# Two transformer blocks on one core: the values products of block 2 turned round, GpSimd remainders cut in quarters, whole heads prepared ahead in block 1

## The chip, the core and the metric

The kernel runs on one NeuronCore of a Trainium2 chip. The metric is the device time of one execution in microseconds (us). TensorE (PE) multiplies matrices, VectorE (DVE) and ScalarE (ACT) do elementwise work and may read PSUM, GpSimd (POOL) does elementwise work on SBUF alone, and SyncE (SP) issues most of the transfers. Matrix products land in eight PSUM banks of 128 partitions by 512 float32 values.

## What is computed

The reference runs two transformer blocks, one after the other, on one sequence of 512 tokens with 1024 channels, in float32. Cut to what matters here:

```python
def first_block(x, ...):
    xn = rmsnorm(x, norm_mix_g)
    proj = xn @ w_in                                   # q, k, v, u, v-gate, forget logits
    att = forgetting_attention(q, k, v, log_f)         # 8 heads of 64, causal
    sg = chunked_spatial_gating(u, vg, ...)
    x = x + concatenate([att, sg]) @ w_out
    return rmsnorm(x + conv_ffn(rmsnorm(x), w_up, conv_w, conv_b, w_down))

def second_block(x, c, positions, ...):
    h = modulate(rmsnorm_2(x, g_attn_norm), sh_a, sc_a)
    q_lat, kv_lat, k_rope, ca_qkv = split(h @ w_in)
    o_mla = mla_attention(q, k, v)                     # 8 heads, keys of 96, values of 64
    o_ca = chunk_attention(cq, ck, cv, rel_bias)       # 8 heads of 64
    x = x + g_a * (concatenate([o_mla, o_ca]) @ w_out)
    ...                                                # a convolutional feed-forward part
```

In both blocks a head's attention is a softmax over the scores of 512 queries by 512 keys of which a causal part is allowed, and its product with v:

```python
s = einsum('bqhd,bkhd->bhqk', q, k) * scale + bias     # masked
p = softmax(s)
o = einsum('bhqk,bkhd->bqhd', p, v)
```

## The kernel before

**Products.** Channels stand on the partitions and the 512 tokens along the free dimension. A weight piece of 128 by up to 1024 values is loaded by a transfer (`load_split`, L337), cast by ACT to a rounded high part `whi` (L350), and the rest `wlo` is a subtraction (L351), on DVE, or on POOL for those pieces whose row in the plan says `pool=True`: twelve pieces, of w_u, w_qk and of w_ck1 and w_cv1. A step of a matrix product is then three PE instructions (hi by hi, hi by lo, lo by hi), all recorded at L372 (`mm`).

**Order.** The PE order is that of the code. The other engines' instructions are ordered by priority. The loop `attention()` (L619) runs over steps t; a step is one block of 128 queries of one head (four steps to a head, 32 to the first eight heads of a block). Step t issues the scores of t (`strip_scores`: PE products into a bank `s`, on DVE the bias at L597, on ACT the exponential at L601 into a tile `p`), some background work `bg` for DVE, ACT and POOL, then `fill.run(r / 2)`, then the turn of step t-1 (`strip_turn`: PE transposes of `p` at L610 back into its bank `s`, and one copy to a tile `pt` at L612, on an engine of the scheduler's choice, `nc.any`), `fill.run(r / 2)` again, what `later` holds, and the values of step t-2 (`strip_values`). `fill` is a list of jobs of PE work (the weight products of the neighbouring parts); `rate(t)` says how many nanoseconds of it go beside step t. Where fill has run dry, the steps follow each other without it.

**Values.** For a block of queries, `strip_values` multiplies for every block of keys the 128x128 block of `pt`, as stationary operand, with 64 columns of v: 1, 2, 3 and 4 products for the four steps of a head, into a 64-column piece of the bank `o`, which a pair of heads share. After a pair, `pair_end` (L709) divides by the sums (L715, L717, on DVE), and in the next step PE transposes the result into a bank `s` (L725), and `split` (L741 on ACT, L742 on DVE) makes of it one of the eight pairs `mix` that the output product `w_out` reads. Each head of 64 channels has its q and k as `qs`, `kh`, `kl` tiles with high and low halves stacked on the partitions (`stack_q`, `stack_k`; the second halves of kh and kl are copied by two transfers on SP, L700).

**Block 1** (L1266, `head`): a head's preparation comes in four slices, spread over the steps before its first. On POOL stand there the remainders `wlo`, the gelu of the gating part (L1111, L1112), its squares (L1124), the mask `cm` (L1277) and the gains (L1138). **Block 2** (`block2_mix`, L1361): eight heads of the chunked attention (`ca_head`, v in `vc`), then eight of the latent attention (`mla_head`, v in `vm`). The fill there is, in order, cq1, ck1, mla0, cv1, mla1, out0, out1 and the output's tail; its products leave PSUM by `nc.any` copies (L1462, L1463, L1469, L1521, L1526, L1597). Normalizing of q and k (`ca_norm` with the multiply L1457, `q_norm`, `k_norm`, `rope`) is background work. `gemm_tm`, `weave` and `then` make jobs of products and evacuations. PSUM banks: in block 1 three `s`, one `o`, four `mm`; in block 2 the same numbers.

Of the kernel before, what the change touches and what calls it, by code (L numbers as in the profile page):

```python
# [236 lines left out]
class Kernel:  # L237
# [99 lines left out]
    def load_split(self, src, pool, dest, skew):  # L337
# [281 lines left out]
    def attention(self, heads, fill, rate, bg, bgrate, mix, depth=1):  # L619
# [21 lines left out]
        for t in range(n + depth + 3):  # L641
            r = rate(t)
            if t < n:
# [3 lines left out]
                for h in range(len(heads)):  # L647
# [5 lines left out]
            u = t - depth  # L653
            if 0 <= u < n:
                h, qi = seq[u]
                pt[u] = self.strip_turn(hd[h], qi, sc.pop(u))
            if t > n + depth:
# [3 lines left out]
            fill.run(r / 2)  # L661
            for f in later:
                f()
            later = []
            u -= 1
            if 0 <= u < n:
                h, qi = seq[u]
                if u % 8 == 0:
                    o = self.bank("o")
                ov = 2 * qi + h % 2  # L670
                self.strip_values(hd[h], qi, pt.pop(u), o[:, ov * 64:(ov + 1) * 64])
                if h < last:
                    if u % 8 == 7:
                        later = [self.pair_end(o, mix, *hd[h]["end"])]
                elif u % 4 == 3:
                    later = [self.pair_end(o, mix, *hd[h]["end"], half=u % 8 // 4)]
# [12 lines left out]
    def stack_k(self, tiles, k, odd, scale=None):  # L689
        nc, (_, kh, kl) = self.nc, tiles  # L690
        a, b = HALF_P[::-1] if odd else HALF_P
        if scale is None:
            nc.scalar.copy(kh[a], k[a])
            nc.vector.tensor_tensor(out=kl[a], in0=k[a], in1=kh[a].bitcast(F32), op=ALU.subtract)
        else:
            nc.scalar.activation(out=kh[a], in_=k[a], func=AF.Copy, scale=scale[a])
            nc.vector.scalar_tensor_tensor(out=kl[a], in0=k[a], scalar=scale[a], in1=kh[a].bitcast(F32),
                                           op0=ALU.mult, op1=ALU.subtract)
# [10 lines left out]
    def pair_end(self, o, mix, sums, at, pool, tag, half=None):  # L709
# [12 lines left out]
        def turn():  # L722
# [6 lines left out]
            ins = self.split(mix[at], tp, c512)  # L729
            if half:  # L730
# [996 lines left out]
```

## Time and profile before

| | us |
|---|---|
| median of 3 runs | 1227.69 |
| lowest and highest | 1226.39, 1227.93 |
| the profiled execution, own time | 1225.62 |
| its span in the profile | 1223.9 |
| PE busy | 1193.0 (97%) |
| DVE busy | 780.2 (64%) |
| ACT busy | 526.5 (43%) |
| POOL busy | 190.5 (16%) |

The profiled execution took 1.7 us more than its span, and lies 2.1 us below the median of the three runs. The granted clock of TensorE is 0.997 of full speed over the span, so one level holds throughout. A busy share of PE counts overlapping records once.

### The profile page before, as it was taken

The numbers are of one execution on the slowest core, as the hardware profiler recorded it, in microseconds if no ns is written. First come the engines' busy times: TensorE is split into PE (matmuls) and PEld (weight loads), VectorE is DVE, ScalarE is ACT, GpSimd is POOL, SyncE is SP. The second block draws the span as 40 slices with busy tenths as digits, with TensorE's granted clock in tenths as the row PEclk, the third lists the DMA queues.
The fourth block names the chain that finished last, engine by engine and source line by source line (L and its number), as shares of the span: only waits on it lengthen the run. The fifth ranks groups of instructions, "written<-read, shape, count | busy, mean of one in ns | idle before, by whom it ended". The sixth has DMA issues, their size and how long they took to land.

```text
span 1223.9 us, 17406 instructions
## 1 busy us (share of the span) xinstructions
PE 1193.0 (97%) x6730; PEld 1038.9 (85%) x6730; DVE 780.2 (64%) x1392; ACT 526.5 (43%) x946; POOL 190.5 (16%) x209
## 2 busy tenths in 40 slices
PE   9999898999999999999998989999999999999998
PEld 6898688988888888888998988899988888888887
DVE  6646777688888887433575878876675665653221
ACT  6535445454444443323434556655544444442110
POOL 2367301300000000000245472301200000000000
PEclk9999999999999999999999999999999999999999
DMA  7432222166666666433121333111133323233330
GB/s 237 120 102 78 82 82 61 53 188 196 200 192 190 193 190 190 144 98 128 58 86 57 87 109 104 36 36 36 53 123 102 103 86 104 93 89 112 114 110 18
DMA packets 42594, 135.78 MB, mean 111 GB/s; under 512 B 5120, under 2 KB 6016, under 8 KB 42512
## 3 DMA queue, kind: packets, MB, share of 16 engines
q1 hardware_dynamic: 34096, 106.84, 28.3%
q10 hardware_dynamic: 8208, 27.27, 7.4%
q8 instruction: 52, 0.85, 0.3%
q0 software_dynamic: 208, 0.57, 0.2%
q14 instruction: 30, 0.25, 0.1%
HBM read 128.37 MB, written 2.10 MB: 107 GB/s over the span
## 4 chain that ended last, share of the span: by engine, by line
PE 84%; DVE 6%; POOL 4%; issue 2%; ACT 2%; DMA 1%; SPq 0%; ACTq 0%; DVEq 0%; POOLq 0%
PE mm L372 74%; PE s L372 4%; PE o L372 3%; PE s L610 2%; POOL wlo L351 1%; ACT whi L350 1%; DVE wlo L351 1%; DVE s L597 1%; DVE ca L1457 1%; DMA x<-in_xT_dram 1%; POOL gelu L1111 0%; PE mm L1667 0%; DVE nt L557 0%; ACT p L601 0%; PE s L725 0%
## 5 line engine op out<-in xcount | busy, mean ns | idle before, releaser
L351 DVE TENSOR_TENSOR wlo<-wraw,whi 128x1024 fp32r<-128x1024 f32 (+4 forms) x182 | 210.3, 1157 | 180.6 <-ACT whi L350 179.5
L372 PE MATMUL mm<-xnh,whi 128*128 128x512 f32 (+1 forms) x832 | 310.8, 374 | 5.6 <-DVE x L877 2.7
L350 ACT CAST whi<-wraw 128x1024 fp32r<-128x1024 f32 (+4 forms) x194 | 191.6, 991 | 277.8 <-PE mm L372 260.2
L372 PE MATMUL mm<-xnl,whi 128*128 128x512 f32 (+1 forms) x832 | 309.7, 372 | 0.0
L372 PE MATMUL mm<-xnh,wlo 128*128 128x512 f32 (+1 forms) x832 | 309.7, 372 | 0.0
L372 PEld LDWEIGHTS mm<-xnh,whi 128*128 128x128 f32 x832 | 156.2, 188 | 33.5 <-DVE x L877 2.9
L372 PEld LDWEIGHTS mm<-xnh,wlo 128*128 128x128 f32 x832 | 156.1, 188 | 27.6
L372 PEld LDWEIGHTS mm<-xnl,whi 128*128 128x128 f32 x832 | 156.2, 188 | 26.7
L372 PE MATMUL mm<-gh,whi 128*128 128x512 f32 (+1 forms) x384 | 141.3, 368 | 1.1 <-DVE x L967 0.6
L372 PE MATMUL mm<-gh,wlo 128*128 128x512 f32 (+1 forms) x384 | 141.1, 367 | 0.0
L372 PE MATMUL mm<-gl,whi 128*128 128x512 f32 (+1 forms) x384 | 141.0, 367 | 0.0
L759 DVE SCALAR_TENSOR_TENSOR cv<-mm,cols,cv 128x510 f32<-128x510 f32 (+1 forms) x176 | 130.3, 745 | 2.5 <-ACT cv L757 0.5
L372 PE MATMUL mm<-whi,xnh 128*128 128x256 f32 (+3 forms) x304 | 96.5, 318 | 1.1 <-ACT xnh L842 1.1
L372 PE MATMUL mm<-wlo,xnh 128*128 128x256 f32 (+3 forms) x304 | 93.6, 308 | 0.2 <-DVE wlo L351 0.2
L372 PE MATMUL mm<-whi,xnl 128*128 128x256 f32 (+3 forms) x304 | 93.6, 308 | 0.1
L372 PEld LDWEIGHTS mm<-gh,whi 128*128 128x128 f32 x384 | 72.1, 188 | 13.5 <-DVE x L967 0.8
L372 PEld LDWEIGHTS mm<-gh,wlo 128*128 128x128 f32 x384 | 72.1, 188 | 12.1
L372 PEld LDWEIGHTS mm<-gl,whi 128*128 128x128 f32 x384 | 72.1, 188 | 12.0
L601 ACT ACTIVATE p<-s,st 128x128 f32<-128x128 f32 (+1 forms) x96 | 50.7, 528 | 70.4 <-DVE st L597 64.6
L1028 DVE CUSTOM_DVE_ANT_0 wada<-wada,cs,cols 128x1024 f32<-128x1024 f32 x48 | 61.5, 1282 | 28.9 <-DMA wada<-in_w_ada_dram 28.8
L372 PE MATMUL mm<-mix,whi 128*128 128x256 f32 (+1 forms) x288 | 73.8, 344 | 2.6 <-DVE x L877 1.5
L757 ACT ACTIVATE cv<-mm,cols 128x512 f32<-128x512 f32 x88 | 67.6, 773 | 0.0
(296 smaller groups left out, 1793.2 us busy)
## 6 DMA issues: line engine op xcount, KB each, us to landing
wraw<-in_w_up_dram SPq DMA_DIRECT2D x88, 512.0 KB, 3.6
wada<-in_w_ada_dram ACTq DMA_DIRECT2D x48, 512.0 KB, 3.7
wraw<-in_w_down_dram SPq DMA_DIRECT2D x32, 512.0 KB, 3.6
wraw<-in_w_out_dram SPq DMA_DIRECT2D x16, 512.0 KB, 3.7
wraw<-in_w_down_dram SPq DMA_DIRECT2D x16, 384.0 KB, 3.2
wraw<-in_w_qk_dram SPq DMA_DIRECT2D x8, 512.0 KB, 4.2
wraw<-in_w_v_dram SPq DMA_DIRECT2D x8, 256.0 KB, 4.9
x<-in_xT_dram SPq DMA_DIRECT2D x8, 256.0 KB, 6.5
```

What stands on the lines that cost most here:

```text
L350: nc.scalar.copy(hi[:, :n], raw[:, :n])
L351: (nc.gpsimd if pool else nc.vector).tensor_tensor(out=lo[:, :n], in0=raw[:, :n], in1=hi[:, :n].bitcast(F32), op=ALU.subtract)
L372: self.nc.tensor.matmul(out, lhsT, rhs, start=start, stop=stop, **kw)
L597: self.urgent = nc.vector.tensor_tensor_reduce(out=s[:, cs], in0=s[:, cs], in1=b, scale=1.0, scalar=3e38 if j == 0 else st[:, j - 1:j], op ...
L601: nc.scalar.activation(out=p[:, :nk], in_=s[:, :nk], func=AF.Exp, bias=st[:, len(parts) - 1:len(parts)], scale=-1.0, accum_out=hd["sums"](qi))
L610: self.nc.tensor.transpose(s[:, c], p[:, c], self.ident)
L757: nc.scalar.activation(out=t, in_=ps, func=AF.Identity, scale=w[2], bias=self.col(cb, n))
L759: nc.vector.scalar_tensor_tensor(out=t[:, d:], in0=ps[:, :512 - d], scalar=w[2 - d], in1=t[:, d:], op0=ALU.mult, op1=ALU.add)
L1028: nc.vector.tensor_tensor_reduce(out=w, in0=w, in1=self.cs, scale=1.0, scalar=self.col("b_ada_2", n), op0=ALU.mult, op1=ALU.add, accum_out ...
L1457: nc.vector.tensor_tensor(out=v3, in0=v3, op=ALU.mult, in1=ss[:, j, z, t].unsqueeze(2).to_broadcast([P, 4, 64]))
```

## The change

There are four parts. First, a POOL remainder is cut into pieces of 256 columns: the twelve instructions become 48. Second, in block 2 (`side=True`) the values of a pair of heads are multiplied together when both heads' `p` are turned: now v is the stationary operand (64 columns) and the transposed p moves, with 512, 384, 256 and 128 columns for the four blocks of keys; the first head's result goes to partitions 0 to 63 of the bank `o`, the second's to 64 to 127, and the two heads' products alternate. The result stands already transposed; what has to be transposed now is the row of reciprocals, which `side_end` spreads on ACT, turns on PE into a bank `mm`, and copies on ACT, after which DVE multiplies and the split follows. All copies `pt` and all evacuations of products in block 2 are set on ACT. Third, the rates of block 2 are others, three rounds of fill and background stand before its attention, `final` is queued behind mla1, and `pt2` has two buffers (of 13 blocks) in place of three, `stk2` nine in place of twelve. Fourth, in block 1 a head is prepared as a whole, two steps ahead and at high priority, and its `stack_k` computes the second halves on ACT and DVE, so that its 16 transfers fall away.

```diff
-            (nc.gpsimd if pool else nc.vector).tensor_tensor(
-                out=lo[:, :n], in0=raw[:, :n], in1=hi[:, :n].bitcast(F32), op=ALU.subtract)
+            step = 256 if pool else n
+            for o in range(0, n, step):
+                c = slice(o, min(o + step, n))
+                (nc.gpsimd if pool else nc.vector).tensor_tensor(
+                    out=lo[:, c], in0=raw[:, c], in1=hi[:, c].bitcast(F32), op=ALU.subtract)
...
+    def side_turn(self, pt, qi, sp):
+        nk = (qi + 1) * P
+        s, p = sp
+        for kb in range(qi + 1):
+            c = slice(kb * P, (kb + 1) * P)
+            self.nc.tensor.transpose(s[:, c], p[:, c], self.ident)
+        self.nc.scalar.copy(pt[:, qi:4 * qi + 1:3], s[:, :nk].rearrange("p (k q) -> p k q", q=P))
+
+    def pair_values(self, hds, pts, o, half=None):
+        q0, q1 = (0, 4) if half is None else (2 * half, 2 * half + 2)
+        for kb in range(q1):
+            a = max(q0, kb)
+            for z, (hd, pt) in enumerate(zip(hds, pts)):
+                p = pt.rearrange("p a b -> p (a b)")[:, (3 * kb + a) * P:(3 * kb + q1) * P]
+                self.mm(o[HALF_P[z], a * P:q1 * P], hd["v"](kb), p, kb == 0, kb == q1 - 1)
...
+            if ahead:
+                with self.tc.high_priority(offset=AHEAD):
+                    for h, _ in seq[:t + ahead + 1]:
+                        slices(h)
...
             fill.run(r / 2)
...
+            if side:
                 for f in later:
                     f()
                 later = []
...
+                u = t - depth
+                w = u - 1
+                if 0 <= w < n and w % 8 == 7 or n - 8 <= w < n and w % 4 == 3:
+                    h = seq[w][0]
+                    half = None if h < last else w % 8 // 4
+                    if not half:
+                        o = self.bank("o")
+                    self.pair_values([hd[h - 1], hd[h]], [pt[h - 1], pt[h]], o, half)
+                    later = [self.side_end(o, mix, *hd[h]["end"], half=half)]
+                if 0 <= u < n:
+                    h, qi = seq[u]
+                    if qi == 0:
+                        pt[h] = self.pt.tile([P, 13, P], F32, tag="pt", name="pt")
+                    self.side_turn(pt[h], qi, sc.pop(u))
+                fill.run(r / 2)
...
         if scale is None:
-            nc.scalar.copy(kh[a], k[a])
-            nc.vector.tensor_tensor(out=kl[a], in0=k[a], in1=kh[a].bitcast(F32), op=ALU.subtract)
-        else:
...
+            for o in (a, b):
+                nc.scalar.copy(kh[o], k[a])
+                nc.vector.tensor_tensor(out=kl[o], in0=k[a], in1=kh[a].bitcast(F32), op=ALU.subtract)
+            return
...
+    def side_end(self, o, mix, sums, at, pool, tag, half=None):
...
+        att = self.att.tile([P, 512], F32, tag="att", name="att")
+        nc.vector.reciprocal(sums[:, c8], sums[:, c8])
+        nc.scalar.copy(att[:, c512].rearrange("p (g d) -> p g d", d=64),
+                       sums[:, c8].unsqueeze(2).to_broadcast([P, 2 * len(qs), 64]))
+
+        def turn():
+            tp = self.bank()
+            for t in qs:
+                nc.tensor.transpose(tp[:, t * P:(t + 1) * P], att[:, t * P:(t + 1) * P], self.ident)
+            if not half:
+                t = pool.tile([P, 2, 512], F32R, tag=tag, name="mix")
+                mix[at] = t[:, 0], t[:, 1]
+            nc.scalar.copy(att[:, c512], tp[:, c512])
+            nc.vector.tensor_tensor(out=att[:, c512], in0=o[:, c512], in1=att[:, c512], op=ALU.mult)
+            ins = self.split(mix[at], att, c512)
...
+            tiles = qs, kh, kl = self.stacked(stk)
+            self.stack_q(tiles, qf[pr], odd)
+            self.stack_k(tiles, kf[pr], odd)
 
             cp = self.bank()
             self.mm(cp, pick[:, h:h + 1].to_broadcast([P, P]), cum, True, True)
...
-                       lambda t: 1300, mix)
+                       lambda t: 1300, mix, ahead=2)
...
-        self.pt = self.pool("pt2", 3, ctx=ctx)
+        self.pt = self.pool("pt2", 2, ctx=ctx)
...
-        stk = self.pool("stk2", 12, ctx=ctx)
+        stk = self.pool("stk2", 9, ctx=ctx)
...
-            yield from self.gemm_tm(i[w], 256, xn, lambda t, ps: nc.any.tensor_copy(out=dst(t), in_=ps), **kw)
+            yield from self.gemm_tm(i[w], 256, xn, lambda t, ps: nc.scalar.copy(dst(t), ps), **kw)
...
-            yield 6000
+            yield 3000
...
+        for _ in range(3):
+            fill.run(1500)
+            bg.run(800)
         self.attention(
             heads, fill,
-            lambda t: 3000 if t < 0 else 2000 if t < 16 else 1600 if t < 34 else 500,
-            bg, lambda t: 1700 if t < 16 else 600, mix)
+            lambda t: 1500 if t < 0 else 1900 if t < 16 else 1600 if t < 34 else 600,
+            bg, lambda t: 1700 if t < 34 else 1200, mix, depth=1, side=True)
```

In the lists of instructions PE's matrix instructions in all go from 6415 to 6323; block 2's values are 160 before and 68 after. ACT's copies go from 448 to 501, DVE's from 46 to 19, and SP's transfers from 251 to 235.

The first place is PE in block 2 where the fourth block of queries of the first pair's second head is due. Before, the values of one step stand there (`o<-vc,pt`, four products with 64 moving columns); the names `wlo`, `whi`, `lath` are those of the latent product in the fill:

```order
L372 MATMUL mm<-wlo,lath 128x384
L372 MATMUL mm<-whi,lath 128x384
L372 MATMUL o<-vc,pt 128x64 x4
L372 MATMUL s<-kh,qs 128x384
L372 MATMUL s<-kl,qs 128x384
L372 MATMUL mm<-whi,lath 128x384
```

After the change the same engine has at that place the whole pair:

```order
L376 MATMUL mm<-wlo,lath 128x384
L376 MATMUL mm<-whi,lath 128x384
L376 MATMUL o<-pt,vc 64x512 x2
L376 MATMUL o<-pt,vc 64x384 x2
L376 MATMUL o<-pt,vc 64x256 x2
L376 MATMUL o<-pt,vc 64x128 x2
L629 MATMUL s<-ident,p 128x128
L376 MATMUL mm<-whi,lath 128x256
```

The pair's twenty products of 64 columns, which stood before in eight places, have become eight products in one place, and the turn of the next pair's first step follows them directly.

The second place is POOL in block 1, where the second half of the gating part meets the remainders. Before, a mask, the gains and whole remainders take turns:

```order
L526 TENSOR_TENSOR ss<-ss,nhalf 128x16
L351 TENSOR_TENSOR wlo<-wraw,whi 128x1024
L1277 TENSOR_TENSOR cm<-ch,cmask 128x512
L351 TENSOR_TENSOR wlo<-wraw,whi 128x1024
L1138 TENSOR_TENSOR uv<-uv,gg_row 128x256
L351 TENSOR_TENSOR wlo<-wraw,whi 128x1024
```

After it:

```order
L355 TENSOR_TENSOR wlo<-wraw,whi 128x256 x4
L530 TENSOR_TENSOR ss<-ss,nhalf 128x16
L355 TENSOR_TENSOR wlo<-wraw,whi 128x256 x4
L1214 TENSOR_TENSOR uv<-uv,gg_row 128x256
L355 TENSOR_TENSOR wlo<-wraw,whi 128x256 x4
```

Four quarters stand where one remainder stood, one remainder has gone ahead of the powers `ss`, and the mask of the head no longer stands between them (its head is prepared elsewhere).

The third place is ACT in the second half of block 2's attention (the latent heads), around the end of a pair. Before the change (`hi` is a high part of a latent head's q or k, `mix` the split behind a pair; copies `pt` that are not in this list stand on DVE):

```order
L601 ACTIVATE p,sums<-s,st 128x384
L741 CAST mix<-s 128x512
L1671 CAST hi<-mm 96x512
L612 COPY pt<-s 128x384
L601 ACTIVATE p,sums<-s,st 128x512
L1674 ACTIVATE hi<-mm,gml 96x512
L601 ACTIVATE p,sums<-s,st 128x128
```

After it (`att` is the tile of reciprocals, spread at L793, turned on PE and copied at L803):

```order
L793 COPY att<-sums 128x512
L605 ACTIVATE p,sums<-s,st 128x256
L630 COPY pt<-s 128x128
L803 COPY att<-mm 128x512
L605 ACTIVATE p,sums<-s,st 128x384
L630 COPY pt<-s 128x2x128
L817 CAST mix<-att 128x512
L1744 CAST hi<-mm 96x512
L605 ACTIVATE p,sums<-s,st 128x512
```

Two instructions `att` for each pair are new on ACT between the exponentials, and each step has its copy `pt` there.

## Rows read from the trace of the kernel before

**Rows 1.** The page: busy time by engine, and the chain that ended last, by engine.

```profile
PE 1193.0 (97%) x6730; PEld 1038.9 (85%) x6730; DVE 780.2 (64%) x1392; ACT 526.5 (43%) x946; POOL 190.5 (16%) x209
PE 84%; DVE 6%; POOL 4%; issue 2%; ACT 2%; DMA 1%; SPq 0%; ACTq 0%; DVEq 0%; POOLq 0%
```

**Rows 2.** PE's waits: engine, line waited for, us in total, times, longest.

```profile
PE s L610 <- ACT p L601: 3.6, 6, 1.3
PE mm L1633 <- DVE ca L1457: 3.4, 2, 2.2
PE mm L1633 <- DVE qs L687: 3.0, 2, 2.7
PE mm L372 <- DVE mix L745: 2.8, 2, 2.6
```

**Rows 3.** Groups by form on PE: busy us, mean ns of one.

```profile
L372 PE MATMUL o<-vc,pt 128*128 128x64 f32 x160 | 21.4, 264 | 0.4 <-ACT pt L612 0.4
...
L372 PE MATMUL mm<-tri,lfh 128*64 128x512 f32 x1 | 0.4, 390 | 0.0
```

**Rows 4.** PE's timeline in block 2: start us, length us, tile; x counts records.

```profile
667.16 0.28 PE L372 MATMUL s<-kh,qs 128*128 128x256 f32 x1
667.28 0.28 PE L372 MATMUL s<-kl,qs 128*128 128x256 f32 x1
...
676.22 0.55 PE L372 MATMUL o<-vc,pt 128*128 128x64 f32 x4
676.58 0.36 PE L372 MATMUL s<-kh,qs 128*128 128x256 f32 x1
676.78 0.28 PE L372 MATMUL s<-kl,qs 128*128 128x256 f32 x1
...
683.97 1.00 PE L372 MATMUL o<-vc,pt 128*128 128x64 f32 x8
684.77 0.42 PE L372 MATMUL s<-kh,qs 128*128 128x384 f32 x1
```

**Rows 5.** PE's timeline in block 1: the gating products in float32, then a wait.

```profile
124.20 1.46 PE L372 MATMUL mm<-uv,wsp 128*128 128x256 f32 x6
125.49 0.49 PE L610 MATMUL s<-ident,p 128*128 128x128 f32 x3
128.28 0.50 PE L372 MATMUL mm<-xnh,whi 128*128 128x512 f32 x1 [2.29 <-DVE kf L1186]
```

**Rows 6.** Stretch of the latent heads: us, busy us of PE, PEld, DVE, ACT, POOL.

```profile
773.00:838.00 65.00, 64.91 (x484) 60.09 (x483) 46.55 (x116) 38.23 (x103) 7.94 (x8) 1.00 0.08 26
```

**Rows 7.** Timeline of one late step, all engines: its scores, exponential, turn.

```profile
818.65 0.28 PE L372 MATMUL s<-hi,lo 96*128 96x256 f32 x1
...
820.05 0.59 ACT L612 COPY pt<-s 128x512 f32<-128x512 f32 x1 [0.80 <-PE s L610]
...
820.53 0.37 ACT L601 ACTIVATE p<-s,st 128x128 f32<-128x128 f32 x1
...
821.17 0.27 PE L610 MATMUL s<-ident,p 128*128 128x128 f32 x1
```

**Rows 8.** Timeline at the start of block 2's attention.

```profile
652.91 5.81 DVE L1457 TENSOR_TENSOR ca<-ca,ssc 128x256 f32<-128x256 f32 x4 [3.01 <-POOL ssc L526]
...
652.95 2.67 POOL L351 TENSOR_TENSOR wlo<-wraw,whi 128x1024 fp32r<-128x1024 f32 x1
...
658.45 1.21 PE L1633 MATMUL mm<-ident,ca 128*128 128x128 f32 x6 [2.17 <-DVE ca L1457]
...
664.90 0.36 PE L372 MATMUL s<-kl,qs 128*128 128x256 f32 x1 [0.20 <-DMA kl<-kl]
```

**Rows 9.** Timeline in block 1: POOL's remainder and a DVE multiply.

```profile
105.67 2.39 POOL L351 TENSOR_TENSOR wlo<-wraw,whi 128x1024 fp32r<-128x1024 f32 x1
105.73 2.60 DVE L1136 TENSOR_TENSOR uv<-uv,ss 128x256 f32<-128x256 f32 x1 [2.10 <-POOL ss L526]
```

**Rows 10.** Timeline of PE in block 2: its longest wait for DVE qs.

```profile
708.79 0.63 PE L1633 MATMUL mm<-ident,ca 128*128 128x128 f32 x4 [2.66 <-DVE qs L687]
```

More of the change, by code (lines that the diff above doesn't have):

```diff
@@ L617, in strip_values, with attention @@
             self.mm(o, pt[:, kb * P:(kb + 1) * P], hd["v"](kb), kb == 0, kb == qi)
-    def attention(self, heads, fill, rate, bg, bgrate, mix, depth=1):
+    def side_turn(self, pt, qi, sp):
[12 more added lines that the diff above has]
+                self.mm(o[HALF_P[z], a * P:q1 * P], hd["v"](kb), p, kb == 0, kb == q1 - 1)
+    def attention(self, heads, fill, rate, bg, bgrate, mix, ahead=None, depth=1, side=False):
         last = len(heads) - 2
@@ L646, in attention @@
                 sc[t] = self.strip_scores(hd[h], qi)
-                for h in range(len(heads)):
+                for h in range(len(heads)) if not ahead else ():
                     if 0 < seq.index((h, 0)) - t <= LEAD:
@@ L660, in attention @@
                 later = []
[L661 to L676, printed above, removed]
+                u = t - depth
@@ new lines, in attention @@
+                fill.run(r / 2)
+            else:
+                u = t - depth
+                if 0 <= u < n:
+                    h, qi = seq[u]
+                    pt[u] = self.strip_turn(hd[h], qi, sc.pop(u))
+                if t > n + depth:
+                    for f in later:
+                        f()
+                    later = []
+                fill.run(r / 2)
+                for f in later:
+                    f()
+                later = []
+                u -= 1
+                if 0 <= u < n:
+                    h, qi = seq[u]
+                    if u % 8 == 0:
+                        o = self.bank("o")
+                    ov = 2 * qi + h % 2
+                    self.strip_values(hd[h], qi, pt.pop(u), o[:, ov * 64:(ov + 1) * 64])
+                    if h < last:
+                        if u % 8 == 7:
+                            later = [self.pair_end(o, mix, *hd[h]["end"])]
+                    elif u % 4 == 3:
+                        later = [self.pair_end(o, mix, *hd[h]["end"], half=u % 8 // 4)]
@@ L1294, in bias @@
                 return r
-            return dict(qk=[(qs, kh), (qs, kl)], bias=bias, v=lambda kb: vv[:, kb, h * 64:(h + 1) * 64], sums=sh,
-                        end=(sums, pr, mx, "mix"))
+            return dict(qk=[(qs, kh), (qs, kl)], bias=bias, v=lambda kb: vv[:, kb, h * 64:(h + 1) * 64],
+                        sums=sh, end=(sums, pr, mx, "mix"))
+            yield
         cumulate()
@@ L1520, in f @@
             def f(t, ps):
-                nc.any.tensor_copy(out=mq[c][t // 2][:, t % 2], in_=ps.rearrange("p (h d) -> p h d", d=QK))
+                nc.scalar.copy(mq[c][t // 2][:, t % 2], ps.rearrange("p (h d) -> p h d", d=QK))
             return f
```

37 lines of the change are left out of this document (16 added, 21 removed).

## The prediction

> **What bounds the kernel now.** I read the page first. PE is busy for 97% of the span, and the chain that ended last runs through PE for 84% of it [rows 1]. So an edit counts for what it takes from PE's own work, or for what it changes in the some 30 us in which PE stands still. I then read the waits of PE: the largest are short and spread out, for the exponential of a step, for the normalizing multiply L1457, for `qs`, for the split L745 [rows 2]. No single wait is worth more than 5 us, so the first question is what PE's own work costs, and the third view is the groups by form: the products `o<-vc,pt` of the first eight heads of block 2 are 160 records, and `o<-vm,pt` has the same [rows 3]. Their mean of 264 ns includes the time in which records overlap, so I took starts from the timeline instead.
>
> There two products (four records: each float32 product leaves two) start at 676.22 and the next instruction at 676.58: .36 us. Four products take .80 (683.97 to 684.77) [rows 4]. So each further product takes .22, one takes .14 and three .58, and a head, with 1, 2, 3 and 4, takes 1.88. Behind such a group the next pair `kh`, `kl` starts .20 apart instead of .12 behind weight products (676.58 to 676.78, against 667.16 to 667.28) [rows 4], so every group costs another .08. A head is 2.20 and block 2's sixteen heads 35.2 us.
>
> **Values turned round.** The nearest row for a float32 product that is bound by its moving columns is the gating product of block 1: six records of 256 columns start at 124.20 and the next work at 125.49, so one record takes .215 and a product (two records) .43, or 1.68 ns for each column [rows 5]. A head moves 512, 384, 256 and 128, 1280 columns: 2.15 us, and a pair 4.30. Eight pairs are 34.4, and nine groups instead of 64 cost .7 in exits: 35.1, a gain of 0.1. Fewer columns of the stationary operand alone bring nothing: the one product of the trace with 64, 128x512, takes 390 ns, the length of a full one [rows 3]. The gain must come from two heads running side by side in the halves of the array. As the heads alternate and each product has two records, the second record of one head could lie beside the first of the other; a pair is then half of 4.30, and one record of 512 columns (.43) more for the stagger, 2.58. Eight pairs with the exits are 21.3, which is 13.9 less than 35.2. The two ends are 0 and -13.9. No row of this trace has two halves of the array at work, so the choice rests on what the order does: the alternating products have different stationary operands, different output partitions and no data in common, which is an arrangement in which the row's 64 idle columns could be used. I take the upper end, -13.9, as likelier than not.
>
> The Trainium skill bears on this on its page "TensorEngine Tiling (Array Packing)", section "Key Properties": different tiles of the array can load and multiply in parallel, but a change of the tiling mode drains the engine. By its first rule the pair is 2.58, by its second each of the nine groups pays twice. No run here shows either. The following sentence prices the second from rows alone. If entering and leaving cost the tail of a record each (length .28 less the step of .12 [rows 4], .16), eighteen changes are 2.9 us; the exits above hold .7 of that, so the forecast would become 2.2 us worse.
>
> **The evacuations, the pt copies and the new ACT work.** In the stretch of the latent heads ACT is busy 38.2 of 65 us and DVE 46.6 [rows 6]. `side_end` adds two ACT instructions of 512 columns for each of four pairs, 8 times .59 ([rows 7], the copy of that size), 4.7; the copies `pt` that DVE has there move over; were they one in five of the 32, that is 3 to 4 by the same .59. ACT then has about 46, DVE about 43. Neither becomes the bound by sums, so these cost nothing in the first half of block 2, where the fill of weight products lies between a step's scores and its turn. In the second half that cover is thin.
>
> **Late steps.** One step there: the last score product starts at 818.65, the exponential at 820.53, behind a copy `pt` that began at 820.05 and takes .59, and the turn at 821.17: 2.5 us, all of which PE filled with other work [rows 7]. In the change a step loses its values as cover (.14 to .80, mean .47, and .08) and gains .1 of fill (600 for 500 ns). PE's six waits for the exponential come to 3.6 us now, the longest 1.3 [rows 2]. I take 1.7 us more for the 30 steps from t=34 on, which is .06 for a step: most have more slack than they lose. To it come three places. The fill runs dry earlier, since three rounds of it were spent ahead: by the order the steps 28 to 33 have none, where it was 30 to 33; two more bare steps at about .6 (the mean of the six waits) are 1.2. The last `mix` is a longer chain: turn of the reciprocals, ACT copy, DVE multiply, ACT cast, DVE subtract, where it was cast and subtract; two more links of about .59 with their hand-over, 1.4, against which about .65 of output products stands: .75. The first half of the last pair has the same chain with less beside it, .8. Together +4.5. Low end 0 (the slack is enough everywhere), high end +12 (.25 for each of the 30 steps on top).
>
> **The start of block 2.** PE waits there 3.4 us for L1457 [rows 2], and .2 for the transfer of `kl` [rows 8]. The four multiplies take 5.81 us while POOL's remainder of 2.67 us runs [rows 8]. In block 1 a single one takes 2.60 beside a remainder of 2.39 [rows 9], so DVE stands until POOL's instruction is over. In the change 42 more records of the weight products, at .12, stand ahead of the transposes: 5 us, enough for both waits. But behind them only 18 records are left, where 30 were, ahead of the first scores. From the last six transposes to `kl` it takes 6.45 us (658.45 to 664.90) [rows 8]; six transposes and 18 records fill about 3.0. So the stall moves to the first scores and is about 3.4: -0.2 in all. Bounds -3.4 and +1.
>
> The Trainium skill gives the reason on its page "SBUF — State Buffer", section "Who interferes with whom": a VectorE instruction with two SBUF inputs and a GpSimd one that reads SBUF exclude each other for a whole instruction. The rows above agree (2.60 beside 2.39).
>
> With quarters the longest such hold is about .6 (2.39 / 4) in place of 2.4. That helps DVE only where a remainder is the holder: at L1457, and in block 1.
>
> **Middle of block 2.** PE's largest single wait there, 2.66 for `qs` at 708.79 [rows 10], comes from a queue of DVE work in which the evacuations stand. They leave DVE (27 copies), and the multiplies of the background are spread over more steps (1700 until t=34). With the neighbouring waits for DVE and for the exponential I count 4 us in reach and take half, -2. Bounds -4 and 0.
>
> **Block 1.** Its waits for `kf` (2.29 at 128.28 [rows 5]) and for the split L745 (2.8 in two [rows 2]), with starved last steps (part of the 3.6 for the exponential), come to about 10. Quarters shorten the hold of DVE in the gating part, and heads prepared two steps ahead spread a run of weight products that no step interrupted. Against it: `kf` is still evacuated behind gelu rows, each head's preparation now comes at once at high priority (five ACT and five DVE instructions, with eight halves of .4 to .5 that were transfers), and what stands behind it on DVE is the bias of a running step. Taking the 16 transfers off SP shortens only the way of `kh` and `kl`; the weight loads behind them on SP come far ahead of use. I take a quarter of the 10, -2.5. Bounds -8 and +3.
>
> The two buffers `pt2` cost nothing: the next pair's first copy follows its turn, which PE issues behind the values that release them. In that place the copy waits for the transposes anyway.
>
> **Sum.** -13.9 + 4.5 - 0.2 - 2 - 2.5 = -14.1. Against the profiled execution's 1225.62 that is 1211.5; that execution lies 2.1 below the median, and what is compared is medians: 1227.7 - 14.1 = 1213.6, so 1214.
>
> **Rivals.** (1) The two halves don't overlap. For it speaks that no row shows them overlapping, and that the row with 64 columns is no shorter. Then the first term is -0.1, the sum -0.3, 1227.4. (2) The end on the other side: the chain of the late steps sets the pace. Without values between turn and scores each of the 30 late steps waits for ACT, whose queue has a copy `pt` and often an `att` copy ahead of the exponential; with one copy of .59 [rows 7] exposed in each it costs 17.7 in place of the 1.7 above, more than the values give even with overlap: 1214 + 16 = 1230. It decides from .53 for each step on ((14.1 + 1.7) / 30). Against it: ACT has 19 of 65 us to spare, and PE's waits for the exponential are few now. (3) Both overlap and the smooth first block: terms at their low ends give 1227.7 - 13.9 - 3.4 - 4 - 5 = 1201.
>
> **How the numbers follow.** What a measurement of this kernel can tell from no change is about .2%, 2.5 us. Forecast, 1207 to 1220: 60%. No overlap, 1222 to 1231: 22%; of this 5 are faster, 11 within .2%, 6 slower. The late chain, 1224 to 1236: 14%; 1, 3 and 10. Better than 1207: 4%. Faster .70, same .14, slower .16. The range leaves out 4 below and the upper part of the late chain: 1207 to 1231.
>
> **What would show it.** The groups `o<-pt,vc` in the timeline: a pair in 2.6 us (right) or 4.3 (rival 1). The waits of PE for `p` from 775 us on: near 5 us, or near 18 (rival 2). At the start of block 2 no wait for L1457, but one of about 3.4 at the first scores. The wait for `qs` near 700 halved. POOL's quarters at .6 to .7 each; at .9 or more the remainders come later than now and PE would wait for `wlo`. The prediction is wrong above all if the pair takes 4.3, or if ACT's queue holds each late exponential by half a microsecond.

## The result: slower by 0.8%

The changed kernel takes 1237.55 us (median of 4 runs, 1236.51 to 1238.94) against 1227.81 of the kernel before (4 runs): a ratio of 1.0082, 95% interval 1.0067 to 1.0096. The forecast was 1214, in a range of 1207 to 1231. The profiled execution took 1236.51 us.

### The profile page after: what moved, and what is told of

It reads as the page before. It is cut to its first block, busy times and chain, and to the rows that moved or that the text cites. A ratio compares the mean times of both kernels' runs of the same rounds, so it can differ in the third digit from the quotient of the medians.

```text
span 1234.6 us, 17036 instructions
## 1 busy us (share of the span) xinstructions
PE 1193.4 (97%) x6546; PEld 1025.0 (83%) x6546; DVE 769.8 (62%) x1373; ACT 547.3 (44%) x999; POOL 201.6 (16%) x245
## 4 chain that ended last, share of the span: by engine, by line
PE 82%; DVE 6%; POOL 4%; ACT 3%; issue 2%; DMA 2%; SPq 0%; ACTq 0%; POOLq 0%; DVEq 0%
PE mm L376 74%; PE s L376 3%; PE o L376 2%; POOL wlo L355 2%; PE s L629 1%; DMA bs<-in_relb_dram 1%; DVE s L601 1%; ACT p L605 1%; ACT whi L350 1%; DMA x<-in_xT_dram 1%; POOL nw L530 1%; DVE wlo L355 1%; DVE nt L561 1%; PE s L614 0%; PE mm L1740 0%
## 5 line engine op out<-in xcount | busy, mean ns | idle before, releaser
L376 PEld LDWEIGHTS mm<-xnl,whi 128*128 128x128 f32 x832 | 156.5, 188 | 27.1
L1104 DVE CUSTOM_DVE_ANT_0 wada<-wada,cs,cols 128x1024 f32<-128x1024 f32 x48 | 61.5, 1282 | 27.1 <-DMA wada<-in_w_ada_dram 27.1
```

The lines of the kernel that those rows point to most:

```text
L376: self.nc.tensor.matmul(out, lhsT, rhs, start=start, stop=stop, **kw)
L1104: nc.vector.tensor_tensor_reduce(out=w, in0=w, in1=self.cs, scale=1.0, scalar=self.col("b_ada_2", n), op0=ALU.mult, op1=ALU.add, accum_out ...
```

## The profile after

PE has as much busy time as before [rows 1], although the turned values shorten its products by some 13 us (worked out under "Why the prediction was wrong"):

```profile
PE 1193.4 (97%) x6546; PEld 1025.0 (83%) x6546; DVE 769.8 (62%) x1373; ACT 547.3 (44%) x999; POOL 201.6 (16%) x245
PE 82%; DVE 6%; POOL 4%; ACT 3%; issue 2%; DMA 2%; SPq 0%; ACTq 0%; POOLq 0%; DVEq 0%
```

The pairs of turned values in PE's timeline (start, length; the first and a late one, and what follows each):

```profile
690.83 0.34 PE L376 MATMUL mm<-wlo,lath 128*128 128x384 f32 x1
691.00 0.34 PE L376 MATMUL mm<-whi,lath 128*128 128x384 f32 x1
691.27 2.37 PE L376 MATMUL o<-pt,vc 128*64 128x512 f32 x16
693.58 0.33 PE L629 MATMUL s<-ident,p 128*128 128x128 f32 x1
...
831.37 2.37 PE L376 MATMUL o<-pt,vm 128*64 128x512 f32 x16
833.68 0.33 PE L629 MATMUL s<-ident,p 128*128 128x128 f32 x1
```

A pair takes 2.31 us. The two halves of the array work side by side, as the forecast had it (2.58), and not 4.3 (pairs with a wait inside or at the lower clock are longer, up to 4.17). So the time was lost elsewhere. I cut block 2's attention at the first scores, at the first scores of the latent heads, and at the last product of `w_out` that reads `mix`. Columns: stretch, length, busy time of PE, PEld, DVE, ACT, POOL, granted clock. First the kernel before, then the changed one:

```profile
664.42:767.13 102.71, 97.62 (x746) 92.76 (x745) 79.88 (x187) 58.50 (x148) 47.05 (x55) 1.00 0.33 92
767.13:856.68 89.55, 88.69 (x680) 82.93 (x679) 66.14 (x167) 52.49 (x136) 15.24 (x19) 1.00 0.11 37
```

```profile
660.88:778.37 117.49, 99.29 (x617) 85.68 (x617) 79.45 (x186) 65.25 (x166) 57.99 (x68) 0.88 0.29 85
778.37:865.57 87.20, 84.67 (x593) 72.54 (x592) 58.14 (x144) 59.49 (x156) 7.64 (x10) 0.98 0.10 31
```

The first stretch, that of the chunked heads, is 14.8 us longer with 129 fewer records of PE; block 1 and its feed-forward part were 4.8 us ahead of the kernel before at its end (589.2 against 594.0 us). The parts add up to the 10.7 us between the two spans: -4.8 in block 1, +1.3 from there to the first scores (with 3.5 us of products moved ahead), +14.8, -2.4 among the latent heads, +1.8 behind them. PE's waits in that first stretch (us in total, times, longest) were 5.1 us in all, of which 3.0 for `qs` [rows 2, 10]; now they are 21, and the largest are:

```profile
PE s L629 <- ACT p L605: 8.2, 6, 4.5
PE s L376 <- ACT pt L630: 5.0, 4, 3.6
PE s L376 <- DMA kh<-kh: 2.8, 1, 2.8
PE mm L376 <- DVE qs L734: 2.0, 1, 2.0
PE s L376 <- DMA kl<-kl: 1.0, 1, 1.0
```

And there is a second payment. The mean granted clock of the stretch is 0.88, where it was 1.00. Around the wait of 3.56 us near 704 the timeline reads, over POOL, DVE, ACT and PE:

```profile
703.98 1.61 POOL L1606 TENSOR_TENSOR sqm<-mqk 128x384 f32<-128x384 f32 x2 [0.67 <-DVE nw L1607]
...
704.84 0.55 DVE L1607 TENSOR_REDUCE nw<-sqm 128x4 f32<-128x384 f32 x1 [0.94 <-POOL sqm L1606]
705.42 0.68 DVE L734 TENSOR_TENSOR qs<-mm,qs 64x512 fp32r<-64x512 f32 x1
...
706.14 0.58 ACT L733 CAST qs<-mm 64x512 fp32r<-64x512 f32 x1 [1.66 <-DVE qs L734]
...
707.17 0.48 ACT L630 COPY pt<-s 128x384 f32<-128x384 f32 x1
...
707.71 0.58 PE L376 MATMUL s<-kh,qs 128*128 128x256 f32 x1 [3.56 <-ACT pt L630]
```

and the clock in the stretches of 5 us from there on (same columns as above):

```profile
700.00:705.00 5.00, 3.79 (x32) 3.40 (x30) 3.02 (x7) 3.14 (x7) 4.18 (x10) 1.00 0.25 79
705.00:710.00 5.00, 2.29 (x10) 2.30 (x11) 4.85 (x11) 2.86 (x7) 2.21 (x3) 0.66 0.25 77
710.00:715.00 5.00, 5.00 (x30) 5.00 (x30) 2.54 (x9) 2.80 (x8) 2.91 (x1) 0.66 0.83 232
```

Read it from the top. DVE's reduce of the background waits for POOL's squares. Behind it in DVE's queue stands `qs`, behind that one in ACT's queue the second `qs`, behind that the copy `pt`, and the bank of the next scores is free only when `pt` is copied. One wait for POOL thus stops DVE, ACT and PE in turn. In the whole stretch DVE's waits for POOL come to 16.0 us (6.0 before):

```profile
DVE nw L1607 <- POOL sqm L1606: 3.9, 6, 1.0
DVE mqk L1621 <- POOL nw L530: 3.8, 2, 2.8
DVE ca L1530 <- POOL ssc L530: 3.1, 2, 2.6
DVE ssc L1518 <- POOL sqc L1517: 2.8, 3, 1.8
DVE krs L1632 <- POOL krt L1631: 2.4, 1, 2.4
```

In the ten us from 705 on the mean granted clock is 0.66, a part of the time at the lower level of 1.2 GHz: 3.4 us of full clock were not granted (10 times .34), a little of that during the wait itself. The wait of 4.49 us near 751 ends in DVE's queue too, but there DVE isn't waiting: from 750.5 on it is busy with `final` (L1018), a remainder and an evacuation of the output product, and behind them come the reduces. The exponential waits for a reduce, whose tile of squares takes turns with its own tile `p` in one pool of three buffers:

```profile
753.22 1.65 DVE L1018 SCALAR_TENSOR_TENSOR x<-x,cols,mm 128x256 f32<-128x256 f32 x4
...
754.79 1.46 DVE L1607 TENSOR_REDUCE nw<-sqm 128x4 f32<-128x384 f32 x3
755.37 0.69 ACT L605 ACTIVATE p<-s,st 128x512 f32<-128x512 f32 x1 [3.49 <-DVE nw L1607]
```

## The experiments

The kernel before is timed again beside each group (1228.1, 1227.8, 1227.7, 1228.0 and 1226.8). The fences name the edits in short: against the kernel before in e7 and e13, against the changed one in the others, which in e10 and from e14 on has the pace of before (e6). One number was carried along unmeant: in e1, e5, e6, e8, e10 and e14 to e18 the weight of a job in block 1's gating part is 6000, where both kernels have 3000. It changes PE's order there; block 1 with the heads prepared ahead ends at 589.0 to 589.6 us in e6, e14 and e15, and at 589.0 to 589.4 with 3000 in the change, e2, e3 and e4, so no cost of it shows.

**Which part costs.** Theory A put the loss on ACT's longer queue, theory B on the new pace and the background, theory C on the two-halves products and the clock. First the values alone, and the change without them.

```diff
e1: -  whole heads in block 1, quarters, evacuations on ACT, new pace, final late
    +  as before; only side=True with its buffers stays
e2: -            bg, lambda t: 1700 if t < 34 else 1200, mix, depth=1, side=True)
    +            bg, lambda t: 1700 if t < 34 else 1200, mix)      (and the buffers of before)
```

> Of the change only the turned values of block 2 (with their copies of p and of the reciprocals on ACT and the buffers they need); evacuations, pace, background, block 1 and the remainders are as before. Theory A (the waits come from ACT's longer queue, which the turned values bring with them, and each wait of three us or more is followed by a stretch at the lower clock): the pairs still take about 2.4 us, but waits for ACT appear in the first half of block 2; 1220 to 1232. Theory B (the pace and the background work, not the values, make the waits): the 14 us of the values come through, about 1214. Theory C (the two-halves products themselves lower the clock): a lower clock right behind pairs without any wait, 1230 or more.

> The whole change without the turned values (p stationary as before, pt copies on an engine of the scheduler's choice). Theory A: the waits for the exponential and for copies mostly go, and so does the lower clock; block 1's gain of 4.8 us stays: 1222 to 1227. Theory B: the waits stay and the values' gain is gone: 1245 or more. Theory C: as A, without a lower clock.

The values alone: 1230.98, ratio 1.0021 (1.0010 to 1.0031). The change without them: 1236.53, 1.0067 (1.0052 to 1.0082). The first lies in the range of theory A, and shows no gain from 13 us of shorter products; the second lies in no range, and shows that the rest costs nearly all of the loss. In the profile of the first 2.8 us are lost ahead of block 2's attention already (first scores at 667.2 us, against 664.4), where nothing was meant to change; the clock fell three times in block 1 there (0.68, 0.66 and 0.83 granted in 130:135, 150:155 and 230:240), and not in the profile of before (in that of e13, which has block 1 as it was, it fell twice, at 129 and 149). From the first scores to the last product that reads `mix` it is 3.0 us longer (195.2 against 192.3). The clock is 1.00 in the latent stretch of the first (773.7 to 862.5 us), where five pairs stand, so the two-halves products themselves don't lower it: theory C is out. In the first stretch of that run PE waits for `qs` and for ACT, 13 us in all:

```profile
PE mm L1707 <- DVE qs L734: 5.3, 2, 4.5
PE s L629 <- ACT p L605: 4.1, 3, 2.3
PE mm L376 <- ACT mqk L1601: 2.8, 1, 2.8
```

Then single edits undone in the change.

```diff
e3:  -            else:
     -                bg.add("final", final)     # in mla(1); back behind cq0
e4:  -  nc.scalar.copy(dst, ps)   +  nc.any.tensor_copy(out=dst, in_=ps)   (27 evacuations, pt)
```

> The change with the job called final (the multiply-adds of x at the end of block 1's norm, L1018) put back behind cq0. In the trace of the change they stand on DVE ahead of the reduces L1607, which hold buffers that the exponential needs; PE waits 4.5 us there and runs at the lower clock for some ten us behind. If that is its cause (A, B): 4.5 + 3.4 less, about 1230. If the reduces are held by something else, 1236 to 1239.

> The change with the 27 evacuations and all copies of turned p on an engine of the scheduler's choice again. Theory A (ACT's queue): waits for pt and p in the first half of block 2 shrink by half or more, with their stretches at the lower clock: 1222 to 1230. Theory B (pace and background): 1235 to 1242, since the chain through POOL's squares and DVE's reduces stays.

`final` back: 1232.09, 5.5 us less. Any engine: 1235.66, 1.9 less, which the intervals hardly tell from nothing, and in the range of theory B; ACT's longer queue (theory A) is not the main cause.

**Block 1, and the pace.**

```diff
e5:  only ahead=2, stack_k without transfers, and step = 256
e6:  -        for _ in range(3):
     -            fill.run(1500)
     -            bg.run(800)
     -            lambda t: 1500 if t < 0 else 1900 if t < 16 else 1600 if t < 34 else 600,
     -            bg, lambda t: 1700 if t < 34 else 1200, ...
     +            lambda t: 3000 if t < 0 else 2000 if t < 16 else 1600 if t < 34 else 500,
     +            bg, lambda t: 1700 if t < 16 else 600, ...     (final and rope as before too)
```

> The kernel before with block 1's part (whole heads two steps ahead, second halves of kh and kl computed) and the remainders in quarters, nothing else of the change. In the trace of the change block 1 is 4.8 us shorter. Theory A and D (below) alike: 1222 to 1225. If the lead was eaten later (weights not yet loaded, block 2's start): 1227 to 1229.

> The whole change, but with the pace of before: no rounds ahead of block 2's attention, the old rates of fill and background, final and the rope's weight as before. Theory D (from the first scores to the latent heads, DVE, ACT and POOL set the pace with background work, so that time saved on PE there returns as waits, and more background beside each step makes it worse): the values' waits of the run with values alone remain, block 1's 4.8 us are kept: 1223 to 1228. Theory A (ACT's longer queue): 1232 or more, since the evacuations stay on ACT.

Block 1 alone: 1223.88, 0.9962 (0.9948 to 0.9976). The change with the old pace: 1223.04, 0.9968 (0.9954 to 0.9981). So the new pace, `final` included, costs 14.5 us of 1237.55; without the turned values it costs 12.7 (1236.53, where block 1 alone has 1223.88), the evacuations on ACT included. The first stretch with the old pace, same columns as above:

```profile
658.74:762.28 103.54, 94.92 (x647) 84.36 (x647) 73.62 (x173) 65.87 (x168) 48.66 (x60) 0.96 0.31 91
```

It is 14 us shorter with 30 records more. PE's waits in it are 12.1 us (20.9 with the new pace), DVE's waits for POOL 8.4 (16.0), and by the mean clock some 4 us at full clock were not granted (0.04 of 103.5), where it had been 14 (0.12 of 117.5).

The next two asked whether the background's squares make the chain.

```diff
e7, e8: -  nc.gpsimd.tensor_tensor(out=sq, in0=v, in1=v, op=ALU.mult)
        -  nc.vector.tensor_reduce(out=s2[:, t], in_=sq, axis=AX.X, op=ALU.add)
        +  nc.vector.memset(s2, float(d))
```

> The kernel before, but the sums of squares of the latent heads' q and k and of the second half of the chunked heads' q and k are left out (constants stand for them): 8 squares on POOL and 8 reduces on DVE for the first, 24 altogether. The output is then another. Theory D: PE's waits of 2.7 and 1.4 us near 706 and 722 us shrink, 1222 to 1226. Theory A: no difference, 1226 to 1229.

> The turned values alone, with the same squares and reduces left out as in the run beside it. Theory D: with the background's chain shortened the saving on PE comes through in part: 6 us or more under the run beside it (1216 to 1220). Theory A: as far above it as the values alone were above the kernel before, 1228 to 1232.

Both were slower, 1236.06 and 1240.15, outside every range. Theory D in that form isn't borne out: with those squares gone PE's longest wait for `qs` is still 2.7 us (4.0 with the values). But the runs are a poor test, since the edit also moved work ahead of the attention, where a new wait for POOL's `rstd` of 3.3 and 4.7 us ends near 616.

```diff
e9, e10: -  sq = self.pp.tile([P, 512], F32, tag="p", name="sqm")     (rt and krt likewise)
         +  sq = bgp.tile([P, 512], F32, tag="bg", name="sqm")
e11:     -  bg, lambda t: 1700 if t < 34 else 1200    +  bg, lambda t: 1700 if t < 16 else 600
e12:     -  the three rounds; 1500 if t < 0           +  3000 if t < 0
```

> The whole change, with one buffer of their own for the background's tiles (squares, the rope's products), which before take turns with the exponential's tiles p in a pool of three. Theory P (with the new pace the background stands closer to the exponentials, its tiles hold p's buffers until a chain over POOL and DVE ends, the exponential waits for the buffer, PE for the exponential, and the clock falls behind the wait): the wait of 4.5 us near 751 and the stretch at the lower clock behind it go, 1226 to 1231. Theory A (ACT's queue) or a pace that is too slow for DVE and POOL altogether: 1235 to 1240.

> The change with the pace of before (the run at 1223.0) and the background's own buffer. Theory P: part of the 12 us of waits between the first scores and the latent heads go, 1216 to 1220. If at the old pace the background doesn't hold p's buffers long: 1221 to 1225.

> The whole change, with the rate of background work as before alone (1700 until step 16, then 600, where the change has 1700 until step 34, then 1200). Theory P: the squares and the rope fall back behind the exponentials that they held up, 1226 to 1231. If the three rounds ahead of the attention or final cost the most: 1234 to 1238.

> The whole change without the three rounds of fill and background ahead of block 2's attention and with 3000 instead of 1500 of fill before its first step. The wait for kh and kl at the first scores (3.7 us in the change) then is as in the kernel before, the total there the same: 1235 to 1238 if the start costs nothing by itself; under 1232 if spending the fill early is what leaves the later steps without cover.

Own buffers: 1236.47 and 1224.69, nothing gained. Theory P fell as well: the exponential no longer waits for a buffer, but its bias does stand behind the reduce in DVE's queue. In the first of these two runs, near 702:

```profile
701.99 0.82 POOL L1607 TENSOR_TENSOR sqm<-mqk 128x384 f32<-128x384 f32 x1
702.84 0.55 DVE L1608 TENSOR_REDUCE nw<-sqm 128x4 f32<-128x384 f32 x1 [3.03 <-POOL sqm L1607]
...
705.11 0.57 DVE L601 CUSTOM_DVE_ANT_0 s<-s,bs 128x384 f32<-128x384 f32 x1
...
705.76 0.58 ACT L605 ACTIVATE p<-s,st 128x384 f32<-128x384 f32 x1 [6.36 <-DVE st L601]
...
707.24 0.58 PE L376 MATMUL mm<-whi,lath 128*128 128x256 f32 x1 [5.73 <-ACT att L803]
```

The old background rate alone: 1227.86, 9.7 us less than the change; that is theory P's range, but not by P's buffer, as the two runs above show. The old start alone: 1229.15, 8.4 less, in the range that stood for the fill spent too early; but that edit takes away rounds of fill and of background together, so which of the two costs isn't shown. With the 5.5 of `final` that is 23.6, more than the 14.5 of all of them together, so the parts don't add. In the first stretch PE's waits hardly shrink in these three (17.3, 19.5 and, with `final` back, 22.7 us, against 20.9); more of the gain there is clock (0.92, 0.92 and 0.90 granted, against 0.88).

**Waits and the clock, and what the values' gain became.**

```diff
e13: +  nc.tensor.transpose(ps[:, 0:P], self.ident, self.ident)
     +  nc.scalar.copy(d, ps[:, 0:P])
     +  for _ in range(n):                   # n = 2, 6, 10, 16 at four places
     +      nc.scalar.copy(d, d)
     +  nc.tensor.transpose(ps[:, P:2 * P], d, self.ident)
e14: +  for _ in range(2):
            self.pair_values([hd[h - 1], hd[h]], [pt[h - 1], pt[h]], o, half)
e15: -  self.stack_k(stacks[h + y], ps, y, gca)
     +  self.stack_k(stacks[h + y], ps, y, gca, pr == 0 and y == 0)   # both halves, no transfer
e16: -  step = 256 if pool else n    +  step = n
```

> The kernel before with four waits of PE put into block 2's feed-forward part, where the clock is at its upper level throughout: PE turns a tile, ACT copies it 3, 7, 11 and 17 times in a row (about .25 us each), PE goes on behind the last copy. The result doesn't change. Theory G (a wait of some three us or more is paid twice, since PE runs at the lower level for some time behind it): the first wait of about 1 us costs itself, the longest of about 4.5 us costs itself and 3 to 4 us more; in all 1243 to 1250. If waits alone don't lower the clock (the drops come from what else runs there): the sum of the waits, 1238 to 1241.

> The change with the pace of before (1223.0), and each pair's products of the turned values issued twice in a row, the second time over the first. That is 8 times some 2.4 us, 19 us, more of PE's work, and the same result. Theory W (between the first scores and the latent heads PE waits for chains over POOL, DVE and ACT whose length doesn't depend on PE, so that what PE saves there returns as waits): of the first three pairs' 7 us at most half shows, and altogether 8 to 14 us are added, 1231 to 1237. If the waits stay where they are, the whole 19 to 20 are added: 1241 to 1244.

> The change with the pace of before, with the second halves of kh and kl of the first head of block 2 computed on ACT and DVE, not moved by transfers. PE waits 3.6 us there for the transfer of kh. If the transfer's time is what is late: 2 us less wait and no lower clock behind it, 1218 to 1221. If ACT and DVE, which alternate on that bank, set the end: 1222 to 1224.

> The change with the pace of before, with POOL's remainders whole again. If the quarters shorten DVE's holds in block 1 and ahead of the first scores: 2 to 5 us slower, 1225 to 1228. If block 1's gain comes from the heads prepared ahead alone: 1222 to 1224.

The four waits alone, in the kernel before: 1255.16. The waits are longer than I meant, 2.15, 3.47, 4.78 and 7.15 us, 17.6 in all; the kernel is 27.1 slower. The first and the last in PE's timeline, and the clock behind each:

```profile
929.80 0.33 PE L794 MATMUL mm<-ident,gap 128*128 128x128 f32 x1 [2.15 <-ACT gap L793]
...
1082.40 0.48 PE L794 MATMUL mm<-ident,gap 128*128 128x128 f32 x1 [7.15 <-ACT gap L793]
...
1083.11 0.63 PE L373 MATMUL mm<-xnl,whi 128*128 128x512 f32 x1
1083.53 0.63 PE L373 MATMUL mm<-xnh,wlo 128*128 128x512 f32 x1
```

```profile
930.00:940.00 10.00, 10.00 (x38) 8.11 (x38) 4.33 (x6) 2.35 (x3) 0.00 (x0) 0.83 0.15 52
...
1083.00:1093.00 10.00, 10.00 (x35) 7.94 (x35) 1.23 (x2) 1.72 (x2) 0.00 (x0) 0.74 0.01 2
```

Behind each wait, at once or within 1.5 us, the records start .42 apart (1083.11 to 1083.53) where they had been .23 apart. PE is 100% busy in those ten us, and a wait of 2.15 us costs another 1.7 (10 times .17), one of 7.15 another 2.6; the two between gave 0.83 and 0.82. That is 7.8 on top of 17.6; the rest of 1.7 is not traced. So in four places of four a wait alone was followed by the lower clock, and was paid again with about 2 us (but see the last section).

The pairs twice: 1239.46, 16.4 us more than with them once. The values take 17.3 us longer in PE's timeline (20.8 to 38.1, starts to starts without waits). That is between the two ranges, and against theory W: nearly all of it shows, and the waits hardly changed (12.1 to 11.1 us in the first stretch). The waits don't shrink when PE has more to do at the pairs' place.

The first head's `kh` and `kl` computed: 1218.64, 4.4 less. The wait for `kh` had been 3.6 us and is 0.6, and the clock stays at 1.00 behind it. Whole remainders: 1221.52, 1.5 less than with quarters, but the intervals overlap (0.9931 to 0.9962, and 0.9954 to 0.9981). The 48 quarters take .81 us each on POOL, 37.4 together (they overlap a little); twelve whole ones took 2.44, 29.3.

**Put together.**

```diff
e17: e15 with step = n
e18: e17 with final behind mla1
```

> The change with the pace of before, the first head's second halves of kh and kl computed, and whole remainders: the two edits that each made the change with the old pace faster (1218.6 and 1221.5 against 1223.0). If they add: 1216 to 1218. If the quarters' loss was noise: 1218 to 1220.

> The same, with final queued behind mla1 as the change has it. With the new pace that place cost 5.5 us. If final costs by its place (its multiply-adds stand ahead of the background's reduces on DVE): 3 to 6 us slower than the run beside it, 1220 to 1224. If it costs only where the background runs fast: within 1 us, or up to 3 us faster, since the wait of 2.5 us for a square on ACT behind the attention is missing in runs that had it late.

1218.02, ratio 0.9928 (0.9908 to 0.9949) to the kernel before: faster than both kernels. It isn't told apart from the run with `kh` computed and quarters (1218.64, 0.9928 too), so the quarters' cost is not shown. With `final` late 1221.68: its place costs 3.7 us with the old background too.

## Why the prediction was wrong

**Values turned round: right.** The two halves overlap; a pair is 2.31 (2.58 forecast). In the run with the values alone they take 20.2 us from start to start, where they took 30.6, and the scores behind them 2.5 less through fewer exits: 13 of the 13.9 forecast. Rival 1 is out. The Trainium skill ("TensorEngine Tiling (Array Packing)", section "Key Properties") has different tiles work in parallel, with which the 2.31 agrees, and a change of tiling mode drain the engine. The 2.9 us that were priced for the changes didn't come: the last record ahead of a pair takes about .1 longer (.27 from 691.00 to 691.27, .17 for the same form before it), .8 for nine groups, and behind a pair nothing shows, as the next product starts .08 behind the turn.

**Block 1: right in direction, too small.** -2.5 forecast, -4.8 in the trace, -3.9 in the time of the run with block 1 alone. It comes from the heads prepared ahead with their second halves computed (the two were not parted): with whole remainders that gain stays (block 1 ends at 588.4 us). The quarters, from which I expected shorter holds of DVE, cost POOL a quarter more time, and no run shows a gain from them.

**The start of block 2: right in place.** No wait for L1457 is left, and the first scores wait 3.7 us for the transfers of `kh` and `kl` (3.4 forecast).

**The middle of block 2: the step that failed.** It said that the evacuations leave DVE, that "the multiplies of the background are spread over more steps (1700 until t=34)", and counted -2. The opposite happened: the stretch became 14.8 longer. 1700 until step 34 is more background beside each step from 16 on (it was 600), not the same spread thinner. It and the three rounds ahead bring the background's reduces and multiplies, which wait for POOL, in front of the bias, `qs` and the reciprocals in DVE's queue. With the old pace the same kernel is 14.5 faster. I had read from the trace how long such work takes, not what stands behind it while it waits.

**The clock: a missing term.** I priced every wait at its own length. I had also taken the mean of 0.997 over the span of the kernel before to mean that one level held throughout, and it didn't: behind the two waits for L1457, 3.4 us in sum [rows 2, 8], the clock was 0.73:

```profile
660.00:665.00 5.00, 4.80 (x31) 4.62 (x30) 2.63 (x4) 3.23 (x4) 0.00 (x0) 0.73 0.37 81
```

In the first stretch of the changed kernel the waits grew by 16 us; by the mean clock (0.88 of 117.5) another 14 us at full clock were not granted, a part of them during waits. PE had some 11.5 us less to do in this stretch (3.5 of products moved ahead, some 8 saved by its three pairs), so what was lost in it is 14.8 + 11.5, about 26: 16 of waits, and by difference about 10 of the lower clock.

**The late steps: too dear.** The sum had +4.5 for them, rival 2 some 16 more. PE's waits for `p` among the latent heads are 0.8 us, where near 5 was forecast and near 18 by rival 2. That stretch became 2.4 us shorter (87.2 against 89.6), and of some 4.3 that its values gained about 2 went into waits (0.6 us before, 2.5 now). Behind it PE waits 2.5 for a square on ACT, which the forecast didn't have. PE did wait for `p` and `pt` of ACT, but among the chunked heads, and in the two places shown ACT was itself waiting for DVE. That the time came out beyond even rival 2's 1230 is thus no point for it.

**What stays open.** With the old pace the values and the evacuations on ACT together still gain only .8 (1223.04 against 1223.88 with block 1 alone), which isn't told from nothing. PE's waits from the first scores on were 8.3 us without them and 17.7 with them: 12.1 against 7.1 in the first stretch, 3.1 against .6 in the latent one, 2.5 against .6 behind it, at a square on ACT. That the small products, two or three of them between a chain's start and its end, had been its cover, and that one block of 2.3 us in every eighth step covers nothing else, fits this and the run with the pairs twice; but no run spread the pairs over the steps, so it is argued and not shown.

## What to carry to other kernels

When background work is set to run earlier or faster, look in each engine's queue at what stands behind an instruction that waits for another engine, and not at busy shares: DVE was busy 68% of that stretch and still held up PE. Don't price a wait of PE at its length alone, but look at the granted clock behind it: the four waits of 2.15 to 7.15 us that were put in alone cost 1.7 to 2.6 us more each. Undo a bundle's parts one by one: here block 1's part gained 4 us, the turned values took 13 us off PE's products, of which next to nothing reached the time, and the pace lost 14.5. A version with the old pace, whole remainders and the first head's `kh` and `kl` computed runs at 0.9928.

## What the runs showed that I had not expected

The same wait at the same place, with the same instructions up to there, was followed by the lower clock in one execution and not in another. In block 1 PE waits 2.72 us for `x` in the profile of before and 2.68 in the run without squares; the stretches behind it:

```profile
230.00:235.00 5.00, 4.65 (x39) 4.65 (x40) 3.30 (x4) 0.42 (x1) 0.72 (x1) 1.00 0.40 105
```

```profile
230.00:235.00 5.00, 4.34 (x20) 4.34 (x21) 3.60 (x5) 0.67 (x2) 0.72 (x1) 0.50 0.36 92
```

At the wait the second execution was .4 us behind the first, at the first product of the feed-forward part's down projection 3.1. A single profile therefore says of a wait that it may be paid twice, not that it is.
